# Turning new keys and queries in 32 by 32 blocks on VectorE, and storing them in 128 B runs from ScalarE's queue, in a three-branch mixer layer

## The chip, the cores and the metric

The kernel runs on one core of one Trainium2 chip. The metric is the device time of one execution in microseconds; less is better. Times of the kernel before are the median of three runs.

## The reference, cut to what matters

One layer is computed for two groups of rows: 2048 prompt tokens and 8 sample sequences of 16 tokens. The rows are normalised, projected by one wide matrix into fifteen column segments, go through three branches, and are merged.

```
h = rms_norm(x, norm_g)
(a_x, a_b, a_c, a_z, g_q, g_f, g_i, g_z, s_q, s_k, s_v, s_z, m_a, m_b, m_c) = split_cols(h @ w_in)
o_a = short gated convolution of a_x, a_b, a_c, a_z
o_b = gated linear recurrence of g_q, g_f, g_i, g_z
q = rms_norm(s_q.reshape(B, T, 8, 64), q_norm_g)
k = rms_norm(s_k.reshape(B, T, 8, 64), k_norm_g)
o_c = stick-breaking attention of q, k, s_v (causal), gated by silu(s_z)
m = sigmoid(m_a) * (o_a @ wb_a) + sigmoid(m_b) * (o_b @ wb_b) + sigmoid(m_c) * (o_c @ wb_c)
y = x + m @ w_out;   k and v are outputs too
```

The change is about `q` and `k`, between their normalisation and the attention that reads them: 8 heads of 64 channels for each token.

## The kernel before, in words

**Tiles and groups.** The 17 tiles of 128 tokens (tile 0 is the sample rows, 1 to 16 the prompt) are worked off in three groups of 5, 6 and 6 tiles (`GROUPS`). In each group every column segment of the input projection is one job. Most jobs are by channel (`proj_chan`, line 710: 24 matmuls of 128x384 or 128x256 into one PSUM tile `acc`); keys, queries, values and the recurrence's values are by token (`proj_tok`, line 721: 24 matmuls of 128x256 for each tile of 128 tokens and each half `s` of four heads). Every fp32 product is three matmuls of high and low parts, which the function `split` makes: ScalarE rounds a tile to its high part (line 175), VectorE subtracts that from the tile and leaves the low part (line 176).

**Order of work.** Python generators set the program's order by a cost clock; a scheduling layer then places each engine's instructions in one queue for each engine, which is worked off in order. `ps_acc` gives two buffers for `acc`: TensorE fills one while the other is emptied by ScalarE.

**Keys and queries.** After each by-token tile of `sk` or `sq`, `post_qk` empties `acc` with two ScalarE instructions (`sq`, line 812, and `kn`, line 814), VectorE and GpSimd make the normalising factor, and later VectorE multiplies it and the gain in (lines 819 and 820). There are 17 tiles, two halves and two kinds (key, query): 68 calls. What follows waits in a list, by cost and not by events:

```
    def start_late(gen):
        late.append([next(gen), gen])

    def run_late(cost):
        for x in late:
            x[0] -= cost
```

A generator whose rest is used up goes on to its next `yield`. `LATE = (5.0, 6.0)` are the two rests; a half of a by-token tile costs 1.3 on this clock. In the last step TensorE turns the 128x256 tile `kn` in two 128x128 transposes (line 826) into PSUM (`tp` in the first group, the single buffer `hg` in the others), `split` writes the parts to `kt` (two buffers), and two DMAs on SyncE's queue (SP) store them to the DRAM tensors `KT` and `QT`, in runs of 512 B: 128 partitions by two pairs of heads by 128 tokens.

**Readers.** The prompt's attention loads 64 channels by up to 512 tokens (`load_step`, lines 281, 282 and 287); the sample rows' attention loads tile 0 whole (line 404). They run beside the second and third groups and the merge, as background generators that the cost clock admits between matmuls.

**Queues.** All plain DMAs are issued by SP. The layer that places waits gives every DMA one of eight completion semaphores (`DMAHW0` to `DMAHW7` in the rows below) in turn; a row in brackets is what an instruction waits for. The pools for `kn` (five buffers, shared with the values' `vf`) and `kt` are in `qk`.

Of the kernel before, what the change touches and what calls it, by code (L numbers as in the profile page):

```python
# [8 lines left out]
F32 = mybir.dt.float32  # L9
F32R = mybir.dt.float32r  # L10
# [6 lines left out]
P = 128  # L17
# [9 lines left out]
NTOK = NT * P  # L27
# [16 lines left out]
LATE = (5.0, 6.0)  # L44
# [54 lines left out]
def trunk(ctx: ExitStack, tc: tile.TileContext, x_prompt, x_sample, cache_conv, state_hgrn, cache_k, cache_v,  # L99
# [3 lines left out]
    nc = tc.nc  # L103
# [37 lines left out]
    def ps_tp(dt=F32):  # L141
        return pst[0].tile([P, 512], dt, tag="tp", name="tp")
# [4 lines left out]
    def ps_hg(dt=F32):  # L147
        return pst[0].tile([P, 512], dt, tag="hg", name="hg", bufs=1)

    KT = dram.tile([4, 2, P, NTOK], F32R, name="KT")
    QT = dram.tile([4, 2, P, NTOK], F32R, name="QT")
    VV = dram.tile([NTOK, 8, 64], F32, name="VV")

    OX = dram.tile([3, 4, 2, P, NTOK], F32R, name="OX")
# [16 lines left out]
    def split(hi, lo, src, eng=None):  # L173

        first = nc.scalar.copy(hi, src)  # L175
        return first, (eng or nc.vector).tensor_tensor(lo, src, hi.bitcast(F32), ALU.subtract)  # L176
# [91 lines left out]
    def load_step(m):  # L268

        if m >= len(steps) or m in held:  # L270
            return
        qi, pair, si, _, b0, b1, e = steps[m]
        qb = QBLOCKS[qi]
        h, nb = 2 * pair + e, b1 - b0
        q0, n = qb[0] * P, len(qb) * P
        if si == 0:
            Q1 = at.tile([P, 512], F32R, tag=f"Q1{e}", name="Q1", bufs=1)
            Q2 = at.tile([P, 512], F32R, tag=f"Q2{e}", name="Q2", bufs=1)
            for v in range(2):
                part = QT[pair, v, 64 * e:64 * e + 64, q0:q0 + n].bitcast(F32)  # L280
                nc.sync.dma_start(Q1[64 * v:64 * v + 64, :n].bitcast(F32), part)
                nc.sync.dma_start(Q2[64 - 64 * v:128 - 64 * v, :n].bitcast(F32), part)
        else:
            Q1, Q2 = held[m - 2][0:2]
        Kt = at.tile([P, 512], F32R, tag="Kt", name="Kt")
        for v in range(2):
            nc.sync.dma_start(Kt[64 * v:64 * v + 64, :nb * P].bitcast(F32),
                              KT[pair, v, 64 * e:64 * e + 64, (1 + b0) * P:(1 + b1) * P].bitcast(F32))
        if e == 0:
            Vt = at.tile([P, 4, 2, 64], F32, tag="Vt", name="Vt")  # L290
            nc.sync.dma_start(Vt[:, :nb], VV[(1 + b0) * P:(1 + b1) * P, h:h + 2].rearrange(
                "(b p) e c -> p b e c", p=P))
        else:
            Vt = held[m - 1][3]
        held[m] = (Q1, Q2, Kt, Vt)
# [93 lines left out]
    def sample_attention():  # L389
# [9 lines left out]
        def whole(src, name):  # L399

            part = []
            for v in range(2):
                x = sa.tile([P, 4, P], F32, tag="cst", name=name, bufs=3)
                nc.sync.dma_start(x, src[:, v, :, S0].rearrange("h p t -> p h t").bitcast(F32))
                part.append(x)
            return part

# [401 lines left out]
    def post_qk(acc, t, s, gain, dst, rows_out, first_group):  # L809
# [11 lines left out]
        if rows_out is not None:  # L821
            nc.sync.dma_start(rows_out[:, s * 256:(s + 1) * 256], kn.rearrange("p h d -> p (h d)"))
        yield LATE[1]
        tp = ps_tp() if first_group else ps_hg()
        for j in range(2):
            nc.tensor.transpose(tp[:, j * P:(j + 1) * P], kn[:, 2 * j:2 * j + 2].rearrange("p h d -> p (h d)"), idf)  # L826
        kt = qk.tile([P, 2, 2, P], F32R, tag="kt", name="kt", bufs=2)
        split(kt[:, 0], kt[:, 1], tp[:, :256].rearrange("p (j t) -> p j t", j=2))
        for v in range(2):
            nc.sync.dma_start(dst[2 * s:2 * s + 2, v, :, t * P:(t + 1) * P].rearrange("j p t -> p j t").bitcast(F32),  # L830
                              kt[:, v].bitcast(F32))

    def post_v(acc, t, s):
        vf = qk.tile([P, 256], F32, tag="kn", name="vf", bufs=5)
# [697 lines left out]
```

## Time and profile before

| | us |
|---|---|
| median of three runs (2876.0 to 2877.55) | 2877.0 |
| the profiled execution's own time | 2876.11 |
| its span on the core | 2873.2 |

| engine | busy us | share of the span |
|---|---|---|
| TensorE matmuls (PE) | 2853.0 | 99% |
| VectorE (DVE) | 1546.5 | 54% |
| ScalarE (ACT) | 1018.7 | 35% |
| GpSimd (POOL) | 331.8 | 12% |

A page of the profile gives busy time by engine, then groups of instructions: line, engine, operation, tiles written and read, shape, count, and behind the bar the busy time in us, the mean duration in ns, and the engine's idle time just before with what ended it. PEld is TensorE's weight load, which runs beside its matmuls. A timeline row is start, duration, engine, line, operation; matmuls are pipelined, so that their durations overlap. The granted TensorE clock was 1.00 throughout.

### The profile page before, as it was taken

The page shows a single profiled execution, that of the slowest core. Times are in us where ns is not written, and L with a number is a line of the kernel's source. Part 1 is how long each engine was busy: PE and PEld are TensorE (multiplying, and loading weights), DVE is VectorE, ACT ScalarE, POOL GpSimd, SP SyncE. Part 2 cuts the span into 40 slices and gives each one's busy share as a digit, 9 for nine tenths or more (in the row PEclk, how much of TensorE's full clock was granted, in tenths as well). Part 3 has the DMA queues.
Part 4 walks back from the last instruction along what each step waited for, and adds up shares of the span by engine and source line. Part 5 has one row for each costly group of instructions (what it writes and reads, how often), then busy time and mean ns, then how long its engine had stood idle before and what let it go on. Part 6 is the DMA issues. An engine that isn't in the chain of part 4 may idle for free.

```text
span 2873.2 us, 51723 instructions
## 1 busy us (share of the span) xinstructions
PE 2853.0 (99%) x19479; PEld 2662.3 (93%) x19479; DVE 1546.5 (54%) x3304; ACT 1018.7 (35%) x2375; POOL 331.8 (12%) x802
## 2 busy tenths in 40 slices
PE   9999999999999999999999999999999999999999
PEld 9999999999999999999999999999998888787888
DVE  5454635641344442545434747557485876867743
ACT  4333222242233332213334444434444444544420
POOL 3110000111200000001323111111010011010100
PEclk9999999999999999999999999999999999999999
DMA  8887777777678887746766454544447877878876
GB/s 306 305 276 247 231 241 244 231 243 243 212 249 266 276 265 243 243 167 192 237 215 202 146 173 136 173 139 151 144 145 238 286 234 239 266 250 266 271 250 210
DMA packets 370475, 649.76 MB, mean 226 GB/s; under 512 B 33481, under 2 KB 246306, under 8 KB 339506
## 3 DMA queue, kind: packets, MB, share of 16 engines
q1 hardware_dynamic: 369458, 644.36, 68.2%
q8 instruction: 154, 2.52, 0.4%
q0 software_dynamic: 768, 2.10, 0.2%
q14 instruction: 95, 0.78, 0.1%
HBM read 447.06 MB, written 199.27 MB: 225 GB/s over the span
## 4 chain that ended last, share of the span: by engine, by line
PE 76%; DVE 2%; DMA 2%; issue 1%; ACT 0%; POOL 0%; SPq 0%; DVEq 0%; POOLq 0%; ACTq 0%
PE acc L710 33%; PE acc L721 10%; PE acc L1440 9%; PE acc L1471 6%; PE pv L359 4%; PE tp L310 4%; PE z L330 2%; PE z L329 2%; PE z L1039 1%; PE tp L458 1%; DMA gate<-GM 1%; PE pv L522 1%; PE z L476 0%; PE hg L1086 0%; PE hg L826 0%
## 5 line engine op out<-in xcount | busy, mean ns | idle before, releaser
L710 PE MATMUL acc<-hx,w 128*128 128x384 f32 (+1 forms) x6816 | 1251.8, 333 | 0.1
L710 PEld LDWEIGHTS acc<-hx,w 128*128 128x128 f32 x6816 | 1106.5, 188 | 21.9 <-issue 15.2
L721 PE MATMUL acc<-w,hx 128*128 128x256 f32 x2544 | 328.6, 284 | 1.8 <-DVE hx L176 0.9
L342 DVE TENSOR_TENSOR_SCAN pr<-snb,carry 128x513 f32<-128x513 f32 x192 | 246.5, 1284 | 153.3 <-ACT snb L333 151.7
L721 PEld LDWEIGHTS acc<-w,hx 128*128 128x128 f32 x2544 | 310.9, 188 | 5.0 <-DVE hx L176 1.7
L311 ACT COPY aT<-tp 128x512 f32<-128x512 f32 (+2 forms) x320 | 167.6, 524 | 375.2 <-PE tp L310 361.3
L710 PE MATMUL acc<-hx,wst 128*128 128x384 f32 x1248 | 247.2, 344 | 0.0
L1440 PE MATMUL acc<-o,w 128*128 128x512 f32 (+2 forms) x1080 | 234.7, 363 | 1.8 <-DMA o<-OX 1.8
L333 ACT ACTIVATE snb<-z 128x512 f32<-128x512 f32 (+2 forms) x320 | 172.4, 539 | 144.5 <-PE z L330 140.4
L710 PEld LDWEIGHTS acc<-hx,wst 128*128 128x128 f32 x1248 | 215.4, 188 | 6.4 <-issue 3.7
L1440 PEld LDWEIGHTS acc<-o,w 128*128 128x128 f32 x1080 | 185.1, 188 | 33.8 <-issue 5.3
L347 DVE TENSOR_TENSOR sp<-sp,pr 128x512 f32<-128x512 f32 (+2 forms) x320 | 195.3, 611 | 29.2 <-POOL sp L338 3.7
L342 DVE TENSOR_TENSOR_SCAN pr<-snb,one 128x129 f32<-128x129 f32 (+3 forms) x128 | 114.4, 894 | 123.9 <-POOL snb L338 123.6
L310 PE MATMUL tp<-idf,sp 128*128 128x128 f32 x1088 | 171.3, 273 | 2.5 <-ACT aT L311 1.5
L335 ACT ACTIVATE sp<-z 128x512 f32<-128x512 f32 (+2 forms) x320 | 171.5, 536 | 0.0
L1471 PE MATMUL acc<-w,mh 128*128 128x256 f32 x816 | 161.2, 285 | 1.0 <-DVE yt L1479 0.8
L1176 ACT ACTIVATE gm<-acc 128x384 f32<-128x384 f32 (+1 forms) x144 | 68.2, 474 | 230.4 <-PE acc L710 197.5
L310 PEld LDWEIGHTS tp<-idf,sp 128*128 128x128 f32 x1088 | 131.8, 141 | 19.3 <-issue 4.4
L176 DVE TENSOR_TENSOR w<-wst,w 128x1024 fp32r<-128x1024 f32 x72 | 88.1, 1223 | 110.7 <-ACT w L175 107.9
L1471 PEld LDWEIGHTS acc<-w,mh 128*128 128x128 f32 x816 | 131.0, 188 | 7.2 <-issue 4.2
L329 PE MATMUL z<-Kt,Q 128*128 128x512 f32 (+2 forms) x320 | 128.8, 403 | 0.3 <-ACT sp L335 0.2
L359 PE MATMUL pv<-aT,Vt 128*64 128x512 f32 (+3 forms) x640 | 128.1, 535 | 0.0
(299 smaller groups left out, 3570.1 us busy)
## 6 DMA issues: line engine op xcount, KB each, us to landing
w<-W SPq DMA_DIRECT2D x168, 1024.0 KB, 6.0
W<-w SPq DMA_DIRECT2D x72, 1024.0 KB, 5.0
wst<-W SPq DMA_DIRECT2D x112, 512.0 KB, 5.1
wst<-in_w_in_dram SPq DMA_DIRECT2D x72, 512.0 KB, 5.1
GM<-gm SPq DMA_DIRECT2D x120, 192.0 KB, 3.7
W<-mwp SPq DMA_DIRECT2D x40, 512.0 KB, 4.2
Kt<-KT SPq DMA_DIRECT2D x160, 128.0 KB, 3.1
o<-OX SPq DMA_DIRECT2D x72, 256.0 KB, 4.7
```

The source lines that it names most:

```text
L310: nc.tensor.transpose(tp[:, j * P:(j + 1) * P], sp[:, j * P:(j + 1) * P], idf)
L311: nc.scalar.copy(aT[:, e, 0:nb, i * P:(i + 1) * P], tp[:, :w].rearrange("p (b q) -> p b q", q=P))
L329: nc.tensor.matmul(z[:, :w], Q1[:, i * P:(i + 1) * P], Kt[:, :w], start=True, stop=False)
L333: nc.scalar.activation(sn[:, 512 - w:512], z[:, :w], AF.Sigmoid, scale=-0.125)
L335: nc.scalar.activation(sp[:, :w], z[:, :w], AF.Sigmoid, scale=0.125)
L342: nc.vector.tensor_tensor_scan(pr[:, 512 - w:513][:, ::-1], s_in, s_in, one if diag else carry[e][i], ALU.mult, ALU.bypass)
L347: nc.vector.tensor_tensor(sp[:, :w], sp[:, :w], pr[:, 513 - w:513], ALU.mult)
L359: nc.tensor.matmul(pv[64 * e:64 * e + 64, c0:n], Vt[:, j, e], aT[:, e, j, c0:n], start=first and j == 0, stop=last and j == nb - 1, skip_g ...
L710: nc.tensor.matmul(acc[:, :n], w[0][a][:, k], hT[b][:, k, :n], start=k == 0 and i == 0, stop=k == KB - 1 and i == 2)
L721: nc.tensor.matmul(acc[:, :256], hT[b][:, k, ti * P:(ti + 1) * P], w[k // 4][a][:, k % 4], start=k == 0 and i == 0, stop=k == KB - 1 and i ...
L1440: nc.tensor.matmul(acc[:, :n], w[0][a][:, k, dd * P:(dd + 1) * P], box[x][b][:, k, sl], start=k == 0 and i == 0, stop=k == 3 and i == 2)
L1471: nc.tensor.matmul(acc[:, :256], box["l" if b else "h"][:, k, ti * P:(ti + 1) * P], w[k // 4][a][:, k % 4], start=k == 0 and i == 0, stop= ...
```

## The change

The two TensorE transposes of a call go. VectorE transposes `kn` into the second half of a new tile `kx` in SBUF, block by block of 32 by 32: partition 32a + i, column 32x + j goes to partition 32a + j, column 32x + i. `split` takes its high and low parts from and to SBUF. After that the generator rests once more for `LATE[1]`, and then four DMAs, one for each group `a` of 32 partitions, are issued by ScalarE; each stores 32 partitions by 16 runs (two parts, eight blocks) of 32 tokens, that is 128 B. `kx` takes the tag and the two buffers of `kt`. `KT` and `QT` get a layout in which the 16 runs have one stride, and the readers' indices follow it; the sample rows' loads become eight DMAs where there were four. Lines behind 826 move by one, behind 830 by two: in the changed kernel the matmuls are lines 711 and 722, the transpose is 827 and the stores are 832.

```diff
-    KT = dram.tile([4, 2, P, NTOK], F32R, name="KT")
-    QT = dram.tile([4, 2, P, NTOK], F32R, name="QT")
+    KT = dram.tile([2, 2, 2, P, NTOK], F32R, name="KT")
+    QT = dram.tile([2, 2, 2, P, NTOK], F32R, name="QT")
...
-                nc.sync.dma_start(x, src[:, v, :, S0].rearrange("h p t -> p h t").bitcast(F32))
+                for s in range(2):
+                    nc.sync.dma_start(x[:, 2 * s:2 * s + 2], src[s, v, :, :, S0].rearrange("j p t -> p j t").bitcast(F32))
...
         yield LATE[1]
-        tp = ps_tp() if first_group else ps_hg()
-        for j in range(2):
-            nc.tensor.transpose(tp[:, j * P:(j + 1) * P], kn[:, 2 * j:2 * j + 2].rearrange("p h d -> p (h d)"), idf)
-        kt = qk.tile([P, 2, 2, P], F32R, tag="kt", name="kt", bufs=2)
-        split(kt[:, 0], kt[:, 1], tp[:, :256].rearrange("p (j t) -> p j t", j=2))
-        for v in range(2):
-            nc.sync.dma_start(dst[2 * s:2 * s + 2, v, :, t * P:(t + 1) * P].rearrange("j p t -> p j t").bitcast(F32),
-                              kt[:, v].bitcast(F32))
+
+        kx = qk.tile([P, 2, 256], F32, tag="kt", name="kx", bufs=2)
+        nc.vector.transpose(kx[:, 1], kn.rearrange("p h d -> p (h d)"))
+        split(kx[:, 0].bitcast(F32R), kx[:, 1].bitcast(F32R), kx[:, 1])
+        yield LATE[1]
+        for a in range(4):
+            place = dst[s, :, :, :, t * P + 32 * a:t * P + 32 * a + 32].bitcast(F32)
+            nc.scalar.dma_start(place.rearrange("v j (c q) t -> q (v j c) t", q=32),
+                              kx[32 * a:32 * a + 32].rearrange("q v (x t) -> q (v x) t", t=32))
```

**ScalarE's queue, first group, where the values' tiles (`vf`) follow the keys.** Before, one rounding of turned keys (`kt`) stands with each emptied tile, and no DMA:

```order
L835 COPY vf_1301<-acc_1268 128x256 [waits PE_49]
L175 CAST kt_1296<-tp_1293 128x256 [waits DMAHW6_49,DMAHW7_49,DVE_49,PE_49]
L835 COPY vf_1338<-acc_1305 128x256 [waits PE_49]
L175 CAST kt_1333<-tp_1330 128x256 [waits DMAHW1_49,DMAHW2_49,DVE_49,PE_49]
L835 COPY vf_1367<-acc_1342 128x256 [waits PE_49]
```

These roundings wait for TensorE's transposes and for the two stores of the tile two calls back. The same place now:

```order
L837 COPY vf_1289<-acc_1256 128x256 [waits PE_49]
L832 DMA KT_72<-kx_1205 32x16x32 [waits DMAHW7_49,DVE_49]
L832 DMA KT_72<-kx_1205 32x16x32 [waits DMAHW3_49]
L175 CAST kx_1243<-kx_1243 128x256 [waits DMAHW4_49,DMAHW5_49,DMAHW1_49,DVE_49]
L832 DMA KT_72<-kx_1205 32x16x32
L832 DMA KT_72<-kx_1205 32x16x32 [waits DMAHW6_49]
L837 COPY vf_1326<-acc_1293 128x256 [waits PE_49]
L832 DMA KT_72<-kx_1243 32x16x32 [waits DMAHW7_49,DVE_49]
L832 DMA KT_72<-kx_1243 32x16x32 [waits DMAHW2_49]
L175 CAST kx_1285<-kx_1285 128x256 [waits DMAHW5_49,DMAHW6_49,DMAHW3_49,DVE_49]
```

Between two emptied tiles there now stand four DMAs and a rounding. The rounding of `kx_1285`, which uses the buffer of `kx_1205` again, stands behind two of the four stores of `kx_1243` and less than one tile behind the last store of `kx_1205`.

**VectorE's queue at the same place.** Before, the rows between the gates (`gm`) and the weights (`w`) are the low parts of `kt`:

```order
L1136 TENSOR_TENSOR gm_1259<-acc_1223,gm_1259 128x256 [waits Activation_49]
L176 TENSOR_TENSOR kt_1254<-tp_1251,kt_1254 128x256 [waits DMAHW3_49,DMAHW2_49,Activation_49]
L176 TENSOR_TENSOR w_1263<-wst_1264,w_1263 128x1024 [waits DMAHW7_49,DMAHW1_49,Activation_49]
L176 TENSOR_TENSOR kt_1296<-tp_1293,kt_1296 128x256 [waits DMAHW7_49,DMAHW6_49,Activation_49]
L176 TENSOR_TENSOR kt_1333<-tp_1330,kt_1333 128x256 [waits DMAHW2_49,DMAHW1_49,Activation_49]
```

Each of them is one subtraction behind ScalarE. The same place now:

```order
L176 TENSOR_TENSOR kx_1205<-kx_1205 128x256 [waits Activation_49]
L176 TENSOR_TENSOR w_1251<-wst_1252,w_1251 128x1024 [waits DMAHW5_49,PE_49,Activation_49]
L827 STREAM_TRANSPOSE kx_1243<-kn_1067 128x256 [waits DMAHW5_49,DMAHW7_49,DMAHW4_49,DMAHW1_49]
L176 TENSOR_TENSOR kx_1243<-kx_1243 128x256 [waits Activation_49]
L827 STREAM_TRANSPOSE kx_1285<-kn_1113 128x256 [waits DMAHW6_49,DMAHW7_49,DMAHW5_49,DMAHW3_49]
```

A transpose has come in ahead of each subtraction, and it waits for the four DMAs that store the tile whose buffer it takes.

More of the change, by code (lines that the diff above doesn't have):

```diff
@@ L279, in load_step @@
             for v in range(2):
-                part = QT[pair, v, 64 * e:64 * e + 64, q0:q0 + n].bitcast(F32)
+                part = QT[pair // 2, v, pair % 2, 64 * e:64 * e + 64, q0:q0 + n].bitcast(F32)
                 nc.sync.dma_start(Q1[64 * v:64 * v + 64, :n].bitcast(F32), part)
@@ L287, in load_step @@
             nc.sync.dma_start(Kt[64 * v:64 * v + 64, :nb * P].bitcast(F32),
-                              KT[pair, v, 64 * e:64 * e + 64, (1 + b0) * P:(1 + b1) * P].bitcast(F32))
+                              KT[pair // 2, v, pair % 2, 64 * e:64 * e + 64, (1 + b0) * P:(1 + b1) * P].bitcast(F32))
         if e == 0:
```

## The prediction

> **What bounds the kernel now.** I read the page's engine table first, then the chain that ended last, then who waits on TensorE (the last row is the longest of those waits), then the windows around the keys and queries.
>
> ```profile
> span 2873.2 us, 51723 instructions
> PE 2853.0 (99%) x19479; PEld 2662.3 (93%) x19479; DVE 1546.5 (54%) x3304; ACT 1018.7 (35%) x2375; POOL 331.8 (12%) x802
> PE 76%; DVE 2%; DMA 2%; issue 1%; ACT 0%; POOL 0%; SPq 0%; DVEq 0%; POOLq 0%; ACTq 0%
> PE tp L629 <- DVE xt L619: 2.6, 4, 1.2
> ...
> 140.00:160.00 20.00, 19.71 (x165) 19.35 (x164) 11.52 (x24) 8.14 (x20) 6.00 (x10) 1.00 0.85 285
> 660.00:680.00 20.00, 20.00 (x168) 19.04 (x167) 6.57 (x14) 6.23 (x16) 2.30 (x4) 1.00 0.88 288
> 1420.00:1460.00 40.00, 40.00 (x307) 38.31 (x306) 11.23 (x18) 12.13 (x32) 5.88 (x12) 1.00 0.85 281
> ```
>
> TensorE is the bound: 20 us of the span are left over, and its longest wait in total is 2.6 us, at the start. The window rows (stretch, length, PE, PEld, DVE, ACT and POOL busy, granted clock, DMA share, GB/s) say the same of the three key and query stages, one for each group: PE full, ScalarE 30 to 41% busy, VectorE 28 to 58%, the DMA engines 85 to 88%. So a matmul taken out there is worth its whole time, and whatever keeps a PSUM tile from being emptied costs its whole time. The sum is made against the profiled execution, 2876.11 us (span 2873.2); the median of the three runs, 2877.0, is 0.9 above it.
>
> **What leaves TensorE.** 136 transposes, two for each of 68 calls.
>
> ```profile
> L826 PE MATMUL hg<-idf,kn 128*128 128x128 f32 x96 | 18.3, 272 | 0.0
> L826 PE MATMUL tp<-idf,kn 128*128 128x128 f32 x40 | 7.6, 272 | 0.0
> ...
> 1395.64 1.68 PE L721 MATMUL acc<-w,hx 128*128 128x256 f32 x12
> 1397.15 0.38 PE L826 MATMUL hg<-idf,kn 128*128 128x128 f32 x2
> 1397.29 1.67 PE L721 MATMUL acc<-w,hx 128*128 128x256 f32 x12
> 1399.04 5.86 PE L721 MATMUL acc<-w,hx 128*128 128x256 f32 x48
> ...
> L721 PE MATMUL acc<-w,hx 128*128 128x256 f32 x2544 | 328.6, 284 | 1.8 <-DVE hx L176 0.9
> ```
>
> By the groups they are 18.3 + 7.6 = 25.9 us busy, an upper bound, since ends overlap the next start. The timeline gives the price in place: twelve matmuls and one pair take 1397.29 - 1395.64 = 1.65 us from start to start. In the run of 48 the last end overhangs by about 0.16 (its matmuls last 284 ns), so 5.70 / 47 = 0.121 each, and twelve take 1.45. A pair costs 0.20: 68 x 0.20 = 13.6 us off the path. Nothing waits on the transposes' PSUM buffers today, so their release is put at nothing.
>
> **What comes in, engine by engine.** VectorE gets 68 transposes of 128x256. The trace has none; the nearest rows are its other passes over such a tile.
>
> ```profile
> L820 DVE TENSOR_TENSOR kn<-kn,kg_bc 128x256 f32<-128x256 f32 x34 | 14.4, 425 | 1.0
> 1397.47 0.28 DVE L347 TENSOR_TENSOR sp<-sp,pr 128x128 f32<-128x128 f32 x1
> L347 DVE TENSOR_TENSOR sp<-sp,pr 128x512 f32<-128x512 f32 (+2 forms) x320 | 195.3, 611 | 29.2 <-POOL sp L338 3.7
> L175 ACT CAST kt<-hg 128x256 fp32r<-128x256 f32 x48 | 17.9, 372 | 36.4 <-PE hg L826 36.1 <-DMA QT<-kt 0.3
> ```
>
> I take 0.42, like the pass of the same size, within 0.28 and 0.61 (half and twice the tile): 29 us over three stages where VectorE is 28 to 58% busy, so its own time is covered. The rounding on ScalarE stays 0.37, from SBUF instead of PSUM, and the subtraction stays. GpSimd is untouched. SP loses 136 issues and the waits in front of them; weights and `vf` stores behind them start sooner, worth nothing while PE does not wait for weights. The sample attention's four extra loads and the readers' new indices cost nothing visible: their runs are as long as before. ScalarE gets 272 DMA issues, SP's being the nearest rows (these are of 40 to 180 us, the first group's stage):
>
> ```profile
> L830 SPq DMA_DIRECT2D KT<-kt x20: 359/475/1203, 63.2 to 99.1; - x20
> L830 SPq DMA_DIRECT2D QT<-kt x20: 359/417/1265, 131.8 to 167.9; - x20
> 55.59 0.38 ACT L812 ACTIVATE sq<-acc 128x256 f32<-128x256 f32 x1 [2.20 <-PE acc L721]
> 55.87 0.37 ACT L814 COPY kn<-acc 128x256 f32<-128x256 f32 x1
> 58.44 0.38 ACT L812 ACTIVATE sq<-acc 128x256 f32<-128x256 f32 x1 [2.20 <-PE acc L721]
> 1397.35 0.38 ACT L812 ACTIVATE sq<-acc 128x256 f32<-128x256 f32 x1 [1.06 <-PE acc L721]
> 1410.09 0.38 ACT L812 ACTIVATE sq<-acc 128x256 f32<-128x256 f32 x1 [0.48 <-PE acc L721]
> ```
>
> At 0.42 (0.36 to 1.27) each, four are 1.7 us for every call, and 272 are 114 us of ScalarE. They alone still fit: TensorE hands over a tile every 2.85 us (55.59 to 58.44) in the first group and every 3.19 in the third (1397.35 to 1410.09, four steps); I use 3.0. The copies, the rounding and the issues make 0.65 + 0.37 + 1.7 = 2.7.
>
> **The wait that is added.** ScalarE's order decides. With two `kx` buffers the transpose of call n waits for the landing of all four stores of call n-2, and ScalarE's rounding of call n waits for that transpose. But the stores now come a turn later, so the last of them stands, in ScalarE's own queue, shortly ahead of that rounding: I count 35 of the 68 calls in which only one emptied tile and one or two stores (on average 1.5 us of work) lie between. Behind the waiting rounding stand, in order, the rest of call n-1's stores (2.4 on average) and the next copy out of `acc`, for which TensorE waits. So in these calls one landing is served per tile, and from last store to last store a turn takes
>
> landing + transpose 0.42 + rounding 0.37 + 2.4 x 0.42 = landing + 1.8 us.
>
> What a landing takes (all executions; then `kn` in the three stages, at 40, 600 and 1380 us):
>
> ```profile
> DMA to landing us min/median/max: 1.8/4.1/6.2
> out_dram<-kn SPq DMA_DIRECT2D x34, 128.0 KB, 2.5
> ...
> out_dram<-kn SPq DMA_DIRECT2D x10, 128.0 KB, 2.1
> out_dram<-kn SPq DMA_DIRECT2D x12, 128.0 KB, 3.5
> out_dram<-kn SPq DMA_DIRECT2D x8, 128.0 KB, 3.5
> ```
>
> The first row is that of the old stores (line 830), which stand on SP behind weights of 1 MB; `kn` is a store of the same size that mostly stands alone. The new stores have a queue for themselves, which speaks for 2.5, and move four runs where one was, which speaks for 4.1. Between ends that are equally near I take the middle, 3.3; the bounds are 1.8 and 4.1. A turn is then 5.1 us against 3.0 that TensorE needs: 2.1 x 35 = 73.5. The 35 fall into 15 unbroken runs, and each run may be late by one tile before TensorE stands still, because `acc` has two buffers: 3.0 - 0.65 = 2.35, together 35. That leaves 38.5 us of TensorE standing. Where the third group's attention stands between (two sigmoids), the wait is partly filled, but VectorE, which stands still in the transpose, is then missed by the scans; I let these cancel.
>
> Sum: 2876.1 - 13.6 + 38.5 = 2901.0.
>
> **The DMA engines.** 34816 runs of 512 B become 139264 of 128 B, the bytes staying. In the first group's stage (40 to 180 us), 20 calls, that is 30720 packets more on top of these:
>
> ```profile
> q1 hardware_dynamic: 33892, 42.90, 88.6%
> ```
>
> 88.6% of 16 x 140 us over 33892 packets is 58.6 ns for a mean of 1266 B. A packet of 128 B lies between 5.9 ns (by bytes; then four cost what one did and nothing is added) and 58.6 (nothing saved). The ends are far apart and the row is of far larger packets; I stay near the lower end, and any lateness is in the landing above. In the sum it stands at nothing.
>
> [...]
>
> **The rivals.** First, the landing on the own queue is short, and the kernel gets faster. For it: the old row's minimum is 1.8 and the first stage's `kn` 2.1, and what makes 4.1 of it may be the queue alone. Against it: `kn` itself lands in 3.5 in two of three stages, at a high DMA share, with an eighth of the runs per byte that the new stores have. It decides at a turn where 35 x (turn - 3.0) - 35 = 13.6, so turn 4.4, landing 2.6. At 2.1 the turn is 3.9, the loss 31.5 - 35, nothing, and the time 2876.1 - 13.6 = 2862.5. [...]
>
> Second, both about cancel: landing 2.4 to 2.8, time 2871 to 2883.
>
> Third, the small packets fill the DMA engines. They have 11.4% of 140 us free in the first stage, 16 us. At half the upper bound, 29 ns, the 40960 new packets of its 20 calls take 40960 x 29 / 16 engines = 74 us; the 10240 old ones, by bytes 23.7 ns each, took 15. That is 59 us more, 43 more than is free, and the weights come that much late: 2901 + 43 = 2944. It decides from a packet of 12 ns, where the 16 us are used up. Against it: TensorE waits for no weight there although the DMA share is 0.85 to 0.90 already, and stores may lag where loads may not.
>
> **How the numbers follow.** The wait in ScalarE's queue 0.53; the short landing 0.24; cancelling 0.13; full DMA engines 0.10. The likeliest gives 2901, with a range of its own of 2880 to 2933 (landing 4.1: turn 5.9, 101.5 - 35 = 66.5, less 13.6). The range that should hold it reaches to the fast case and to the third rival: 2862 to 2944. This kernel's measurement tells 0.2%, 5.8 us, from no change. Slower 0.63, same 0.13, faster 0.24.
>
> **What would show it.** TensorE's busy time falls by 14 to 26 us, and rows of PE waiting for ScalarE's copies (`vf`, `kn`, `vg`) appear with some 40 us. VectorE's transposes wait for DMAs into `KT` and `QT` in about 35 calls, ScalarE's `kx` for VectorE. A landing of the 832 stores near 2 us, or a tile cadence that stays at 3.0 in the second stage, proves the first rival; a DMA share of 1.0 from 60 to 170 us with weights awaited, the third. I am wrong if ScalarE's copies are not late behind the rounding.

## The result, and the profile after

| kernel | median us | lowest to highest | runs |
|---|---|---|---|
| before, in the same session | 2876.5 | 2874.98 to 2877.55 | 4 |
| after | 2939.41 | 2933.32 to 2941.28 | 4 |

The ratio is 1.022, interval 1.0207 to 1.0233: 63 us slower. The forecast was 2901, 24.5 us slower; the sign was right, the time is inside the range, and the size is 2.6 times what was forecast. The profiled execution took 2941.28 us.

In the changed kernel's rows the lines from 404 on stand one further on as well: `sq` is 813, `kn` 815, the two multiplications 820 and 821.

From the page after, span, engine table and chain:

```profile
span 2939.6 us, 51642 instructions
PE 2867.5 (98%) x19343; PEld 2667.3 (91%) x19343; DVE 1572.5 (53%) x3372; ACT 1016.9 (35%) x2375; POOL 331.4 (11%) x802
PE 86%; DMA 6%; issue 2%; DVE 2%; POOL 1%; ACT 1%; ACTq 1%; SPq 0%; DVEq 0%; POOLq 0%
```

The windows that stood in the prediction, and two more of the first group's stage:

```profile
140.00:160.00 20.00, 20.00 (x159) 20.00 (x158) 9.86 (x19) 7.76 (x17) 5.77 (x8) 1.00 0.90 285
660.00:680.00 20.00, 19.66 (x146) 18.61 (x145) 4.71 (x11) 4.76 (x13) 2.54 (x5) 1.00 0.89 258
1420.00:1460.00 40.00, 37.22 (x264) 34.64 (x263) 19.93 (x45) 12.37 (x35) 12.14 (x22) 0.96 0.82 226
80.00:100.00 20.00, 16.06 (x104) 15.62 (x105) 10.89 (x26) 8.25 (x20) 4.80 (x8) 0.88 0.65 172
100.00:120.00 20.00, 14.84 (x94) 14.34 (x93) 2.97 (x5) 2.98 (x6) 0.00 (x0) 0.78 0.94 295
```

TensorE stands still for 2939.6 - 2867.5 = 72 us instead of 20, and it is busy 14.5 us longer although 136 transposes are gone. The granted clock, 1.00 throughout before, is 0.88 and 0.78 in the last two windows. Over the span it is 0.993: 0.007 x 2939.6 = 20.6 us lost at most, since TensorE also stood in parts of the slow stretches.

Who waits now. TensorE's waits:

```profile
PE acc L722 <- ACT kn L815: 16.2, 10, 3.4
PE acc L711 <- ACT vr L1129: 7.9, 2, 4.4
PE acc L722 <- ACT vf L837: 6.0, 4, 4.0
```

The view of line 827, VectorE's transposes:

```profile
L827 DVE STREAM_TRANSPOSE kx<-kn x68: 431/445/447, 53.0 to 1622.6; 128x256 f32<-128x256 f32 x68
its engine sat idle before it (us, times) until:
  DMA QT<-kx: 56.2, 13
  DMA KT<-kx: 47.9, 15
...
who waited for it (us, times):
  ACT kx L175: 134.7, 50
```

And of line 832, the stores (duration of an issue, shortest, middle and longest):

```profile
L832 ACTq DMA_DIRECT2D KT<-kx x136: 309/357/2091, 54.4 to 1493.7; - x136
L832 ACTq DMA_DIRECT2D QT<-kx x136: 309/388/2288, 139.9 to 1626.4; - x136
...
DMA to landing us min/median/max: 1.8/3.4/9.1
```

TensorE waits for ScalarE's copies, as forecast: all its waits on ScalarE add up to 48.6 us, against 2.6 before. VectorE's transposes wait 104 us for stores in 28 calls, ScalarE's roundings 135 us for the transposes in 50. One such place in ScalarE's timeline:

```profile
1623.08 0.40 ACT L175 CAST kx<-kx 128x256 fp32r<-128x256 f32 x1 [6.49 <-DVE kx L827]
1623.08 1.41 ACTq L832 DMA_DIRECT2D QT<-kx  x3
1624.53 0.37 ACT L1129 COPY vr<-acc 128x256 f32<-128x256 f32 x1 [1.05 <-issue]
```

And in TensorE's:

```profile
1624.95 4.72 PE L711 MATMUL acc<-hx,w 128*128 128x384 f32 x18 [4.44 <-ACT vr L1129]
```

ScalarE stands 6.49 us in front of a rounding whose transpose is late, then issues three stores in 1.41 us, and only then empties the tile that TensorE has been waiting 4.44 us for.

The clock was not in the forecast. Around a stand of 3.97 us that ends at 113.3, four windows of 3.4 us, then TensorE's timeline:

```profile
105.50:108.90 3.40, 3.40 (x31) 3.40 (x30) 0.00 (x0) 0.00 (x0) 0.00 (x0) 1.00 0.86 236
108.90:112.30 3.40, 0.46 (x4) 0.25 (x3) 0.87 (x2) 0.40 (x1) 0.00 (x0) 1.00 1.06 308
112.30:115.70 3.40, 2.38 (x11) 2.38 (x12) 0.00 (x0) 0.37 (x1) 0.00 (x0) 0.50 1.03 381
115.70:119.10 3.40, 3.11 (x15) 2.81 (x14) 0.45 (x1) 0.38 (x1) 0.00 (x0) 0.50 0.71 164
...
103.79 5.56 PE L722 MATMUL acc<-w,hx 128*128 128x256 f32 x45
113.32 5.49 PE L722 MATMUL acc<-w,hx 128*128 128x256 f32 x24 [3.97 <-ACT vf L837]
```

In the second, TensorE works 0.46 us of 3.4; in the third and fourth the granted clock is 0.50, and 24 matmuls take 5.49 us where 45 of the same shape took 5.56 ahead of the stand. At the earlier pace the 24 would have taken 24 x 5.56 / 45 = 2.97, so the stand of 3.97 us is followed by 2.5 us more. The clock in this trace is 1.00 or 0.50, and the ten slow stretches behind TensorE's stands last 3.41 us (eight of them) or 6.83 us (two), 41.0 in all; the last section lays them beside the stands.

So the span's +66.4 is: transposes gone -13.6, standing +51.9, clock +20.6 at most, and at least +7.5 that is left over and stays unexplained. Taken by TensorE's work in the slow stretches instead of their length (36.6 us of 41.0), the clock is 18.3 and 9.8 are left over.

### The profile page after: what moved, and what is told of

Its sections match the earlier page's. It is cut to its first block, busy times and chain, and to the rows that moved or that the text cites. A ratio compares the mean times of both kernels' runs of the same rounds, so it can differ in the third digit from the quotient of the medians.

```text
span 2939.6 us, 51642 instructions
## 1 busy us (share of the span) xinstructions
PE 2867.5 (98%) x19343; PEld 2667.3 (91%) x19343; DVE 1572.5 (53%) x3372; ACT 1016.9 (35%) x2375; POOL 331.4 (11%) x802
## 2 busy tenths in 40 slices
DMA packets 477164, 649.78 MB, mean 221 GB/s; under 512 B 174985, under 2 KB 352994, under 8 KB 446194
## 4 chain that ended last, share of the span: by engine, by line
PE 86%; DMA 6%; issue 2%; DVE 2%; POOL 1%; ACT 1%; ACTq 1%; SPq 0%; DVEq 0%; POOLq 0%
PE acc L711 43%; PE acc L1442 10%; PE acc L722 8%; PE acc L1473 7%; PE pv L359 4%; PE tp L310 4%; PE z L330 2%; PE z L329 2%; DMA QT<-kx 2%; PE z L1041 2%; DMA KT<-kx 2%; ACTq L832 1%; PE tp L459 1%; PE pv L523 1%; POOL rr L234 1%
## 5 line engine op out<-in xcount | busy, mean ns | idle before, releaser
L711 PEld LDWEIGHTS acc<-hx,w 128*128 128x128 f32 x6816 | 1111.4, 189 | 40.1 <-issue 15.2
L722 PE MATMUL acc<-w,hx 128*128 128x256 f32 x2544 | 337.6, 290 | 27.2 <-ACT kn L815 16.2
L722 PEld LDWEIGHTS acc<-w,hx 128*128 128x128 f32 x2544 | 320.8, 194 | 35.5 <-ACT kn L815 19.8
```

Source lines behind the costliest of these rows:

```text
L711: nc.tensor.matmul(acc[:, :n], w[0][a][:, k], hT[b][:, k, :n], start=k == 0 and i == 0, stop=k == KB - 1 and i == 2)
L722: nc.tensor.matmul(acc[:, :256], hT[b][:, k, ti * P:(ti + 1) * P], w[k // 4][a][:, k % 4], start=k == 0 and i == 0, stop=k == KB - 1 and i ...
```

## The experiments

All differences are to the kernel before in the same session, whose medians lay between 2873.67 and 2876.5. "Standing" is span less TensorE's busy time and "clock" the mean granted clock, both of the profiled execution.

| | median us | ratio, interval | standing us | clock |
|---|---|---|---|---|
| before | 2877.0 | | 20.2 | 1.000 |
| after | 2939.41 | 1.0207 to 1.0233 | 72.1 | 0.993 |
| e1_no_turn | 2931.34 | 1.0182 to 1.0216 | 63.9 | 0.991 |
| e2_sp_queue | 2979.17 | 1.0354 to 1.0389 | 92.2 | 0.988 |
| e3_runs512 | 2922.81 | 1.0151 to 1.0185 | 66.3 | 0.997 |
| e4_bufs3 | 2923.55 | 1.0159 to 1.0193 | 57.9 | 0.994 |
| e5_pe_late | 2885.12 | 1.0022 to 1.0051 | 28.3 | 1.0 |
| e6_dve_now | 2896.12 | 1.0060 to 1.0094 | 44.8 | 0.999 |
| e7_dve_round | 2882.93 | 1.0021 to 1.0041 | 38.3 | 0.998 |
| e8_after_round | 2916.90 | 1.0119 to 1.0160 | 58.6 | 0.995 |
| e9_round512 | 2929.06 | 1.0172 to 1.0206 | 63.9 | 0.993 |
| e10_round_bufs3 | 2910.20 | 1.0112 to 1.0146 | 52.2 | 0.998 |
| e11_round_sp_now | 2989.48 | 1.0381 to 1.0415 | 99.4 | 0.984 |
| e12_round_pool | 2870.68 | 0.9973 to 0.9992 | 27.3 | 0.998 |
| e13_pool_act_round | 2877.93 | 0.9998 to 1.0016 | 32.5 | 0.998 |
| e14_rest_round | 2945.85 | 1.0228 to 1.0259 | 77.5 | 0.991 |
| e15_pool_bufs3 | 2875.14 | 0.9991 to 1.0010 | 30.1 | 0.999 |
| e16_pool_only | 2881.25 | 1.0015 to 1.0034 | 36.7 | 0.999 |
| e17_pool_pad | 2882.34 | 1.0015 to 1.0035 | 33.4 | 0.998 |
| e18_pe_pool | 2894.35 | 1.0050 to 1.0084 | 33.1 | 0.999 |

### First round: one part of the change undone at a time

The theory here, A, was the prediction's own: the stores land late, two buffers make the transposes wait for them, and ScalarE's copies stand behind. Its rivals were the short runs themselves and the issues' place on ScalarE.

**e1_no_turn**, the second rest left out:

```diff
         split(kx[:, 0].bitcast(F32R), kx[:, 1].bitcast(F32R), kx[:, 1])
-        yield LATE[1]
         for a in range(4):
```

> The changed kernel without the second rest: the four stores stay on ScalarE's queue but are issued right behind the low part. In ScalarE's order at least 2.8 us of other work then lie between a call's last store and the rounding that takes its buffer (1.5 us in 35 calls of the changed kernel). Theory A (the rounding waits in ScalarE's queue for a landing, because the stores come late, and TensorE stands and then runs at half clock): VectorE's transposes wait under 30 us for stores (104 us in the changed kernel), TensorE idles under 35 us (72), time 2865 to 2890. Rival B (runs of 128 B fill the DMA engines): nothing changes in packets, time stays above 2920. Rival C (issuing 272 DMAs from ScalarE, with their waits for the eight semaphores, holds the copies): the same issues remain and now wait for VectorE too, time 2905 to 2940.

58 us slower than before, where the change costs 63: the rest is at most some 5 of them (the intervals overlap) and not the cause. Theory A's numbers failed: VectorE's transposes still wait 77 us for stores, not under 30, and TensorE stands 63.9 us, not under 35. Rivals B and C are both still possible.

**e2_sp_queue**, the stores on SyncE's queue:

```diff
-            nc.scalar.dma_start(place.rearrange("v j (c q) t -> q (v j c) t", q=32),
+            nc.sync.dma_start(place.rearrange("v j (c q) t -> q (v j c) t", q=32),
```

> The changed kernel with the four stores on SyncE's queue, still one rest later. Theory A: ScalarE's queue no longer holds the stores behind the waiting rounding, but the rounding still waits for a landing of two calls back; some waits remain: 2875 to 2905. Rival B (small packets): above 2920. Rival C (issues from ScalarE): all of the loss goes, 2860 to 2870.

106 us slower, worse than the change. TensorE's waits change their kind:

```profile
PE acc L711 <- DMA w<-W: 15.4, 2, 10.1
PE acc L722 <- ACT w L175: 13.3, 2, 9.4
```

SyncE's queue loads the weights, and they now stand behind stores. By the number that is rival B's range (above 2920), but the rows show a cause that no theory had; with so large a cost of its own, the run does not price ScalarE's queue.

**e3_runs512**, two stores of 128 partitions in runs of 512 B:

```diff
-        for a in range(4):
-            place = dst[s, :, :, :, t * P + 32 * a:t * P + 32 * a + 32].bitcast(F32)
-            nc.scalar.dma_start(place.rearrange("v j (c q) t -> q (v j c) t", q=32),
-                              kx[32 * a:32 * a + 32].rearrange("q v (x t) -> q (v x) t", t=32))
+        for v in range(2):
+            nc.scalar.dma_start(dst[s, v, :, :, t * P:(t + 1) * P].rearrange("j p t -> p j t").bitcast(F32),
+                                kx[:, v].rearrange("p (j t) -> p j t", j=2))
```

> The changed kernel with two stores of 128 partitions in runs of 512 B in place of four in runs of 128 B, on ScalarE's queue, one rest later; the tile is stored turned block by block only, so keys and queries lie wrongly in memory. The scheduler puts these stores earlier: about 2 us or more lie between a call's last store and the rounding that takes its buffer. Theory A: most waits shrink, 2868 to 2895. Rival B (small packets): all of the loss goes, 2860 to 2866. Rival C (issues from ScalarE): half of the issues remain, about half of the loss: 2895 to 2915.

49 us slower. VectorE's transposes hardly wait for stores now (2.6 and 2.0 us), yet most of the loss stays: short runs are not needed for a loss of this size. The time is above all three theories' ranges. And this kernel loses in another way, which e9 shows.

**e4_bufs3**, three `kx` buffers:

```diff
-        kx = qk.tile([P, 2, 256], F32, tag="kt", name="kx", bufs=2)
+        kx = qk.tile([P, 2, 256], F32, tag="kt", name="kx", bufs=3)
...
-        vf = qk.tile([P, 256], F32, tag="kn", name="vf", bufs=5)
+        vf = qk.tile([P, 256], F32, tag="kn", name="vf", bufs=4)
```

(`kn` and `vr` likewise.)

> The changed kernel with three buffers for the turned tile in place of two (the normalised tiles get four in place of five, to make room). Theory A: the transpose waits for the stores of three calls back, one tile longer in flight: VectorE's waits for stores fall from 104 us to under 30, TensorE's idle time from 72 to under 35, time 2865 to 2890. Rivals B (small packets) and C (issues from ScalarE): packets and issues are the same, above 2915.

The waits for stores fall to 57 us, not under 30, and 13 of the 63 us come back, not 50; the time is in the range of rivals B and C (above 2915). So the third buffer is worth a part; as over half of the wait stayed, this run alone does not price the wait.

### Second round: the parts alone, and the rounding

**e5_pe_late**: the kernel before, its two 512 B stores on ScalarE and a rest later:

```diff
+        yield LATE[1]
         for v in range(2):
-            nc.sync.dma_start(dst[2 * s:2 * s + 2, v, :, t * P:(t + 1) * P].rearrange("j p t -> p j t").bitcast(F32),
+            nc.scalar.dma_start(dst[2 * s:2 * s + 2, v, :, t * P:(t + 1) * P].rearrange("j p t -> p j t").bitcast(F32),
```

> The kernel before with one part of the change: TensorE still turns the block and the two stores keep their runs of 512 B, but they are issued on ScalarE's queue, one rest later. Theory D (what costs the time is ScalarE's rounding standing in its in-order queue until VectorE's chain of normalising and turning is through, with TensorE's copies queued behind it; the stores are second): this kernel has no such chain, since TensorE turns in its own order, so within 15 us of the kernel before, 2865 to 2890 us, TensorE standing 20 to 35 us. Rival E (it is the stores in ScalarE's queue, whose waits for DMA semaphores hold TensorE's copies): 2900 to 2930 us, TensorE standing over 45 us.

10 us slower, inside theory D's range: two issues for each call on ScalarE do little while TensorE turns.

**e6_dve_now**: VectorE turns, ScalarE rounds, and the two stores of e3_runs512 go out at once on SyncE:

```diff
-        yield LATE[1]
-        for a in range(4):
-            ...
+        for v in range(2):
+            nc.sync.dma_start(dst[s, v, :, :, t * P:(t + 1) * P].rearrange("j p t -> p j t").bitcast(F32),
+                              kx[:, v].rearrange("p (j t) -> p j t", j=2))
```

> The other part alone: VectorE turns the 32x32 blocks and ScalarE rounds, but two stores with 512 B runs go out on SyncE's queue at once, without the second rest (their places are then not those of the reference: the keys and queries that attention reads are permuted). Theory D: the cost stays without any store on ScalarE: 2905 to 2930 us, the rounding on ScalarE waiting over 100 us for VectorE. Rival E: with no store on ScalarE the cost is gone, 2860 to 2885 us.

21 us slower, between the two theories' numbers.

**e7_dve_round**: the same, and VectorE makes the rounded half:

```diff
-        split(kx[:, 0].bitcast(F32R), kx[:, 1].bitcast(F32R), kx[:, 1])
+        nc.vector.tensor_copy(kx[:, 0].bitcast(F32R), kx[:, 1])
+        nc.vector.tensor_tensor(kx[:, 1].bitcast(F32R), kx[:, 1], kx[:, 0], ALU.subtract)
```

> The kernel of e6_dve_now with one line more changed: VectorE, not ScalarE, copies the turned block to the rounded half, so that nothing of the block stands in ScalarE's queue (keys and queries permuted as there). Theory D: the copies that free TensorE's accumulators no longer stand behind VectorE's chain; 2855 to 2885 us, TensorE standing under 35 us, granted clock without halved intervals. Rival F (VectorE itself is late: its turning and normalising delay other work of VectorE that TensorE waits for): VectorE has 68 x about 0.3 us more to do, so no better than e6_dve_now, 2905 us or more.

8 us slower than before, 13 faster than e6: inside theory D's range for the time (TensorE stands 38.3 us, a little over its 35), and VectorE has room for 68 passes more.

**e8_after_round**: that edit alone, in the changed kernel.

> The changed kernel with only the rounding moved from ScalarE to VectorE; the four late stores of 128 B runs stay on ScalarE's queue. Theory D: most of the 63 us comes back, what is left is what the stores' waits on ScalarE cost: 2880 to 2915 us. Rival E: 2925 to 2950 us, as the changed kernel. Rival F: over 2940 us.

42 us slower than before, 2 us over theory D's range. What is left is not the rounding on ScalarE.

### Third round: the stores

**e9_round512**: e8_after_round with the two stores of e3_runs512.

> The kernel of e8_after_round (VectorE rounds, stores one rest late on ScalarE's queue) with two stores in runs of 512 B in place of four in runs of 128 B (keys and queries permuted, as in e3_runs512). Theory G (what is left of the cost once VectorE rounds is the four short-run stores: they land late, and the kx buffers and the stores' DMA semaphores are waited for): 2878 to 2895 us, waits of VectorE's transposes for stores under 10 us. Rival H (any store that is issued late on ScalarE's queue costs so much): 2905 to 2925 us, as e8_after_round.

54 us slower, 4 us above theory H's range and more than with the four short stores of e8. The waits of VectorE's transposes for stores are under 10 us, as theory G had it (0.9), but the time is not. The rows show another cause, the order. This is e9's ScalarE queue in the first group; `sq_691` and `kn_693` empty the first tile, `kx_871` is its turned block, and `sq_726` empties the second:

```
L813 ACTIVATE sq_691<-acc_666 128x256 [waits PE_49]
L815 COPY kn_693<-acc_666 128x256 [waits DMAHW5_49]
L832 DMA KT_72<-kx_871 128x2x128 [waits DVE_49]
L813 ACTIVATE sq_726<-acc_701 128x256 [waits PE_49,Activation_49]
L815 COPY kn_728<-acc_701 128x256 [waits DMAHW5_49]
L832 DMA KT_72<-kx_871 128x2x128 [waits DMAHW5_49,DVE_49]
L832 DMA KT_72<-kx_896 128x2x128 [waits DMAHW0_49,DVE_49]
```

In 58 of the 68 calls the first store of a tile stands ahead of the copies of the next key or query tile, although its code comes a rest later: the placing layer has moved it up. So the next tile's copies wait for this tile's whole chain on VectorE. ScalarE's timeline:

```profile
161.94 0.38 ACT L813 ACTIVATE sq<-acc 128x256 f32<-128x256 f32 x1 [3.78 <-DVE kx L829]
162.04 0.38 ACTq L832 DMA_DIRECT2D QT<-kx  x1
162.22 0.37 ACT L815 COPY kn<-acc 128x256 f32<-128x256 f32 x1
```

And VectorE's, from there on:

```profile
162.35 0.42 DVE L817 TENSOR_REDUCE ssq<-sq 128x4 f32<-128x256 f32 x1 [0.46 <-ACT sq L813]
164.18 0.42 DVE L820 TENSOR_TENSOR kn<-kn,rr 128x256 f32<-128x256 f32 x1 [1.41 <-POOL rr L234]
164.64 0.42 DVE L821 TENSOR_TENSOR kn<-kn,qg_bc 128x256 f32<-128x256 f32 x1
165.10 0.45 DVE L827 STREAM_TRANSPOSE kx<-kn 128x256 f32<-128x256 f32 x1
165.58 0.29 DVE L828 CAST kx<-kx 128x256 fp32r<-128x256 f32 x1
165.90 0.42 DVE L829 TENSOR_TENSOR kx<-kx 128x256 fp32r<-128x256 f32 x1
```

From `sq` to the start of the subtraction this round takes 165.90 - 161.94 = 3.96 us, more than the 3.0 in which TensorE fills a tile. Where the round closes in tile after tile, as at the start of the first keys, `sq` follows `sq` by 4.47 and 4.44 us (49.90, 54.37, 58.81). ScalarE's wait for it, `sq` behind line 829, is 133.8 us in 34 calls. e3_runs512 has the same order (turn in the same call, 68 of 68; rounding ahead of the next such tile's copies, 67 of 68), and e6 too (62 and 60). In the changed kernel the placing layer spreads the roundings over up to four such tiles (12 of 68 stand ahead of the next one's copies), so this round is not most of its 63 us.

**e10_round_bufs3**: e8_after_round with the buffers of e4_bufs3.

> The kernel of e8_after_round with three kx buffers in place of two (and four buffers in place of five for kn, vf and vr, for the room). The prediction's own mechanism (a buffer is waited for until the stores of the call before last have landed): 2880 to 2898 us, the 86 us that VectorE's transposes wait for stores mostly gone. Theory J (it is not the buffer but the DMA semaphores that the stores share with the other transfers, waited for on ScalarE ahead of each issue): 2905 to 2925 us.

7 us better than e8 (the intervals overlap), inside theory J's range. But the waits of VectorE's transposes for stores only fell from 86 to 66 us, so a third buffer is again a small part and no clean test of the wait.

**e11_round_sp_now**: e8 without the second rest, stores on SyncE (`nc.sync`).

> VectorE turns and rounds, and four stores in runs of 128 B go out on SyncE's queue at once, without the second rest. Against e7_dve_round (2883, the same with two stores of 512 B runs) it prices the short runs alone. Theory G (short runs land late): the buffers wait, 2900 to 2930 us. If the 136 more issues on SyncE, about 0.4 us each and 54 us in all, are what counts, weight loads come later and it is 2920 to 2975 us, as e2_sp_queue. If neither, 2880 to 2895 us.

114 us slower, the slowest of all and above every range. With e2 it speaks against SyncE's queue, with long waits for weights:

```profile
PE acc L711 <- ACT w L175: 13.1, 3, 10.1
...
PE acc L711 <- DMA w<-W: 11.9, 1, 11.9
```

**e12_round_pool**: as e11, but on GpSimd's queue (the diff is against e8):

```diff
-        yield LATE[1]
         for a in range(4):
...
-            nc.scalar.dma_start(place.rearrange("v j (c q) t -> q (v j c) t", q=32),
+            nc.gpsimd.dma_start(place.rearrange("v j (c q) t -> q (v j c) t", q=32),
```

> As e11_round_sp_now, but the four stores of each block are issued on GpSimd's queue, which is busy 11% of the span: neither ScalarE nor SyncE issues them. This is the version that could beat both kernels. Theory G: the buffer wait stays, but nothing else stands behind it: 2875 to 2905 us. If GpSimd's issue is slow and holds its own work (the rstd that every normalising waits for): 2910 us or more.

4.8 us faster than before, below theory G's range; the interval, 0.9973 to 0.9992, makes it a gain, if one of under 0.2%. TensorE's longest wait in total is 4.8 us, and VectorE's transposes still wait 66 us for landings (35.4 + 30.7), at no price that shows. The 13.6 us of the transposes do not all arrive: TensorE stands 7 us more than before, and up to 5.7 go to the clock.

### Fourth round: settling it

**e13_pool_act_round**: the changed kernel, stores at once on GpSimd's queue, rounding left on ScalarE (e12's diff without e7's).

> The changed kernel with only the stores taken off ScalarE: the four stores of 128 B runs go out on GpSimd's queue without the second rest; the rounding stays on ScalarE. With e12_round_pool (2871) it prices the rounding in ScalarE's queue, with the changed kernel (2939) the stores there. Theory K (each thing left in ScalarE's queue that waits for VectorE's chain holds the copies behind it; the rounding and the stores do so separately): about 10 to 20 us over e12_round_pool, as e6_dve_now was over e7_dve_round, so 2880 to 2895 us. If the stores alone were at fault: 2865 to 2878 us; if the rounding alone: 2920 us or more.

2.6 us over before, within its noise, and 7 over e12. ScalarE's roundings wait as long as ever, and TensorE does not pay (rows of the waits):

```profile
ACT kx L175 <- DVE kx L827: 124.0, 49, 5.6
...
DVE kx L827 <- DMA KT<-kx: 33.5, 14, 4.7
DVE kx L827 <- DMA QT<-kx: 25.9, 12, 6.4
```

This refuted what I had come to believe (theories D and K, that the rounding's wait carries the cost): in this order it is worth 7 us. Nearly all the rest goes with the stores on ScalarE, the second rest still being left out here.

**e14_rest_round**: the changed kernel with one rest more:

```diff
         nc.vector.transpose(kx[:, 1], kn.rearrange("p h d -> p (h d)"))
+        yield LATE[1]
         split(kx[:, 0].bitcast(F32R), kx[:, 1].bitcast(F32R), kx[:, 1])
```

> The changed kernel with one more rest, between VectorE's turn and the rounding on ScalarE, so that the rounding is placed a call later and the turn should long be done when ScalarE comes to it; stores as in the change. Theory K: the rounding's wait for VectorE's turn (135 us in the changed kernel) falls below 40 us, and 10 to 30 us come back: 2905 to 2930 us. If the place of the rounding in ScalarE's queue is not what counts, 2935 to 2950 us.

A miss: 71 us slower than before, the wait 114 us instead of under 40. The rounding did move back in ScalarE's queue, to 4.8 emptied tiles behind its own on average (3.4 in the changed kernel), but the last store of a call moved too (7.1, after 5.3), and the transposes wait 115 us for stores (104): the turn is as late as the rounding.

**e15_pool_bufs3**: e12 with e4's buffers.

> The kernel of e12_round_pool with three kx buffers in place of two (and four in place of five for kn, vf and vr). There VectorE's transposes wait 66 us for landings, without TensorE standing much for it. If that wait costs anything, 2860 to 2868 us; if it is covered, 2868 to 2875 us.

2875.14, no better than e12 and no different from before. VectorE's transposes wait 45 us for stores instead of 66, and the 21 us that went were covered.

**e16_pool_only**: the changed kernel, one word changed, `nc.scalar.dma_start` to `nc.gpsimd.dma_start` in the stores; the rest stays.

> The changed kernel with one word changed: the four late stores are issued on GpSimd's queue in place of ScalarE's; the second rest stays. Theory L (what carries the cost is the stores in ScalarE's queue, as e13_pool_act_round says; the rest is of no account): 2870 to 2885 us. If the missing second rest was what brought e13_pool_act_round down, 2905 us or more.

7 us slower than before, inside theory L's range: of the change's 63 us, 56 go with the stores' queue. Transposes still wait for landings in 29 calls (67.6 us) and roundings 143 us for VectorE, and TensorE hardly pays for either (rows of the waits):

```profile
PE acc L722 <- ACT kn L815: 4.8, 5, 2.1
...
ACT kx L175 <- DVE kx L827: 143.3, 56, 6.6
...
DVE kx L827 <- DMA KT<-kx: 39.0, 17, 5.5
DVE kx L827 <- DMA QT<-kx: 28.6, 12, 4.6
```

**e17_pool_pad**: e13 with four copies on ScalarE where the code had the issues:

```diff
+        yield LATE[1]
+        for a in range(4):
+            nc.scalar.copy(pad, kx[:, 1, 128:])
```

> The kernel of e13_pool_act_round (stores on GpSimd's queue), with four copies of 128x128 of the turned tile into a scratch tile on ScalarE, one rest later, where the changed kernel has its four issues there: about as long each (0.3 us), waiting as those do for VectorE's subtraction, but for no landing. If ScalarE's time and the wait for VectorE are what counts: 2915 to 2945 us, near the changed kernel. If it is the waits for landings of transfers ahead of each issue: 2878 to 2895 us.

6 us over e13 (8 and 2.6 over before). The copies took 0.3 us each and waited for VectorE (the first row, of their line's view, is all 272 of them; the second, of the waits, what they waited):

```profile
L836 ACT COPY pad<-kx x272: 282/299/329, 54.7 to 1564.6; 128x128 f32<-128x128 f32 x136
...
ACT pad L836 <- DVE kx L177: 24.4, 44, 1.9
```

So four times 0.3 us of ScalarE in each call, with some wait for VectorE, do not make the loss. As stand-ins for the issues the copies fall short in two ways: the first of a call stands 3.6 emptied tiles behind the call's own on average, the first issue of the changed kernel 4.6; and they take 81 us in all, where the 272 issues take 144, of which the 53 that last over 0.6 us make 60. Long issues are not ruled out.

**e18_pe_pool**: the kernel before, its two stores on GpSimd's queue (`nc.gpsimd`).

> The kernel before, its transposes on TensorE and its stores in runs of 512 B, with one word changed: the two stores of a block are issued on GpSimd's queue in place of SyncE's. Against e12_round_pool (2871) it says what the turning on VectorE is worth when the queue is the same. The 136 transposes, 0.20 us a pair of them on TensorE, are 13.6 us: so 2868 to 2885 us by that. If what helped e12_round_pool was SyncE's relief and not the turning: 2858 to 2868 us.

20 us slower than before, over both expectations: no gain from SyncE's relief shows, and the rounding waits 51 us for stores there (7 before). With ScalarE rounding and stores on GpSimd in both, turning on VectorE instead of TensorE is worth 2894.35 - 2877.93 = 16 us, though the stores' runs differ between the two.

## Why the prediction was right or wrong

The direction and the place of the loss were right. Two steps failed: a stand of TensorE was priced at its own time alone, with nothing for the clock behind it (up to 20.6 us), and the added wait was put at 38.5 us, where TensorE stood 51.9 us more.

**What leaves TensorE, -13.6: right.** In e12 TensorE is busy 2843.5 us, of which at most 0.002 x 2870.8 = 5.7 are lost clock: 2837.8, 15.2 less than before. The sign named for the changed kernel, a busy time that falls by 14 to 26 us, failed all the same: it rose by 14.5, in the main because slow matmuls are busy for longer.

**What comes in: mostly right.** The transpose took 0.445 (0.42 taken), the rounding from SBUF 0.408 (0.37), both covered as said: e7 even adds 68 passes on VectorE. An issue on ScalarE took 0.357 or 0.388 in the middle (0.42), but up to 2.3 us, and 0.53 on average: 144 us in all, not 114. The sum used a middle value for a thing with a long tail.

**The wait that is added, +38.5: the place was right, the size and a link were not.** Landing 3.4 (3.3 taken), transposes waiting for stores in 28 calls (35 counted), ScalarE's roundings waiting, TensorE waiting for `kn`, `vr`, `vf`: the rows named in advance are there, and TensorE stood 51.9 us more where 38.5 were forecast. That the two figures are near is in part luck. With what was measured (28 calls, a turn of 3.4 + 0.45 + 0.41 + 2.4 x 0.53 = 5.5 us) the prediction's own sum gives some 35 us, so fewer calls and longer issues cancelled, and about 17 us of the standing are outside it.

The link that failed is that the wait for two buffers makes the price. In e16 two buffers and 29 such waits stay and 56 us are gone; e15 takes away 21 us of the wait at no gain; a third buffer in the changed kernel gave back 13 us (e4), in e8 7 (e10). What has to be there are the stores in ScalarE's queue themselves. How they do it is read from the rows and not shown by a run: each waits there for its turn and for landings and runs up to 2.3 us, with TensorE's copies behind it and its own landing, and so the next transpose, late by as much. In e17 plain copies near these places cost 6 us.

The prediction's own bound has a slip too: its upper end, 66.5 less 13.6 over 2876.1, is 2929 and not 2933.

**A term was missing: up to +20.6 for the clock.** "Whatever keeps a PSUM tile from being emptied costs its whole time" is too little: in this trace ten stands of TensorE are followed by 41 us at half clock. In the proportion measured, 20.6 for 51.9, the 38.5 would have become some 54, and the forecast 2916.

**The second rest and the order.** The prediction took the order as given, rightly, and the rest does move a call's last store back by about a tile (5.3 emptied tiles behind the call's own, 4.3 in e1). But this place is not what costs: e1 is only some 5 us faster than the change, and e14, with one rest more, 8 us slower, both at the edge of the noise.

**The rivals.** The short landing is out: 3.4. Cancelling is out. For the third rival, full DMA engines, a packet came out dear enough: queue `q10`, ScalarE's stores, takes 4.1% of 16 x 2939.6 us for its packets, 13.4 ns each, over the 12 from which that rival was to decide.

```profile
q10 hardware_dynamic: 143616, 17.84, 4.1%
```

That is 2.3 times the 5.9 by bytes, and twice what the same bytes take in runs of 512 B (2.1% in e3). But what that rival expects of it did not come: all of TensorE's waits on DMAs in the changed kernel add up to 1.0 us, and e9, without short runs, is still 54 us slower.

**What stays open.** What it is about the stores on ScalarE that costs the 56 us is not divided: their waits for landings ahead of the issue, the long issues, and the shape in which the transfers leave (below) went away together in e16. The traces narrow it. ScalarE's wait for VectorE's transposes stays in e16 (143 us after 135); its stands that end with a store's landing, 42 us in the changed kernel, are gone there, and so are the 144 us of issues. The stands alone do not set the time: e1 has 95 us of them and is no slower than the change. The shape hardly acts outside ScalarE's queue, as the stores land sooner in the changed kernel than in e16 (3.4 against 4.5 us from the issue) and TensorE waits about 1 us for DMAs in both.

## What to carry to other kernels

Before a DMA is put on an engine's queue, ask what stands behind it there: on the engine that empties TensorE's accumulators an issue was here not only its 0.36 us of time (0.53 on average, up to 2.3) but also a place where ScalarE stood until a store had landed, 42 us in all, with the copies that TensorE waits for behind it; and the queue with nothing urgent behind it (GpSimd's, 11% busy) took the same stores for 56 us less. Look for closed rounds, copy to chain to store or rounding to next copy, and compare their length with the time of a tile; a rest in the code does not open one if a later layer moves the instructions up again, as in e9. And to a long stand of TensorE add the slow stretch behind it: here each of the nine steps of 3.41 us with over 1.9 us of standing had one, of 3.41 or 6.83 us at half clock, with up to 1.7 us lost in each 3.41.

## What the hardware did that I had not expected

**The clock.** In the profiled changed kernel the ten slow stretches ahead of the span's end begin and end a whole number of 3.41 us apart. TensorE's work beside them in steps of that length, up to the span's last 7 us: all nine steps at full clock with over 1.9 us of standing were followed by one at half clock, those with up to 1.66 were not, and of two between (1.77 and 1.70) one was. The one of 1.77, which was not, began at 702.8 (the rows cut it to 3.40 us):

```profile
702.80:706.20 3.40, 1.67 (x15) 1.43 (x13) 0.51 (x2) 0.41 (x1) 0.00 (x0) 1.00 0.74 191
706.20:709.60 3.40, 2.00 (x13) 1.52 (x14) 0.91 (x2) 0.98 (x2) 0.00 (x0) 1.00 1.17 305
```

So in this trace each slow stretch had at least 1.70 us of standing, half of a step, in the step ahead of it. The two of 6.83 us went on although TensorE stood only 1.00 and 0.84 us in their first step. The kernel before stands at most 2.2 us in any 3.41 us (from 2179.5 on) and its clock is 1.00 throughout; in steps counted back from the only change of its clock, at 2874.7, behind the span's end, no step ahead of the last 7 us has more than 1.4 us of standing.

**Packets on GpSimd's queue.** The same four stores, 139264 runs of 128 B, make these rows on e12's page:

```profile
DMA packets 342252, 649.78 MB, mean 226 GB/s; under 512 B 35721, under 2 KB 213730, under 8 KB 311282
q0 software_dynamic: 9472, 19.94, 3.4%
```

And in the view of line 832:

```profile
L832 POOL DMA_DIRECT2D KT<-kx x136: 648/649/917, 55.3 to 1434.5; - x136
...
DMA to landing us min/median/max: 2.2/5.0/11.1
```

After had 174985 packets under 512 B; here 35721 are left, and the queue has 9472 - 768 = 8704 packets more than before it took the stores (it had 768), of 17.8 MB, 2 KB each: by the profile's count sixteen runs go as one packet. They land later (5.0 against 3.4 us), and an issue takes 0.65 us of GpSimd, which has them to give.
